# Layer 1's up projection as seven block products instead of eight, from its third pair of column blocks on

## The chip, the cores and the metric

The kernel runs on one core of a Trainium2 chip. The metric is the device time of one execution in microseconds (us). The engines are TensorE (PE, with its weight loads PEld), VectorE (DVE), ScalarE (ACT), GpSimd (POOL) and SyncE (SP), which issues the DMAs. Each has a queue of its own and takes its instructions in the order in which they were written.

## The reference

One step of a network of two layers on 640 tokens (128 context tokens and 512 latent ones), 1024 wide. Each layer is a mixer and then a feed-forward part, which is all that the change touches:

```python
h = rmsnorm(x, p["norm_ffn"]) * (1.0 + sc_f) + sh_f
gate, up = jnp.split(h @ p["w_up"], 2, axis=-1)
x = x + g_f * ((jax.nn.silu(gate) * up) @ p["w_down"])
```

`w_up` is 1024 x 5632 (2816 gate columns, 2816 up columns), `w_down` 2816 x 1024. `sh_f`, `sc_f` and the gate `g_f` come from a small product of a conditioning vector with `ada_w`, one set for the context tokens and one for the latent ones. After layer 1 comes a last rmsnorm, whose result is the output. All is float32.

## The kernel before

**Arithmetic.** A float32 operand is cut into a high part (a rounding copy on ACT) and a low part (a subtraction on DVE). Each product is three matmuls into one accumulator: high by high, high by low, low by high. The normed input of the FFN, transposed, lies in `hT` (high and low, 8 blocks of 128 along k, 640 tokens).

**Weights.** `Stream` brings in one slot of weights after another: `load` is a DMA of up to 512 KB into one of 3 `raw` tiles (L76), `cut` the ACT copy (L86) and the DVE subtraction (L87) into one of 4 pairs `wh`, `wl`. `done` gives a slot back and starts the next cuts and loads.

**Up projection.** `ffn` goes over 22 pairs of column blocks (a gate block and an up block, 128 columns each), in two chunks of 11 pairs in each layer. One block is one slot and 48 matmuls (`ws`, L616): 8 blocks of k, two halves of 320 tokens, 3 matmuls of 128x320. The first three blocks of a layer (L605 to L607) run first over the tokens whose norm is done, then over the rest. A pair ends with ACT's silu (L1080), DVE's product (L1086) and the cut of the result into high and low (L1088, L1089), which makes an `act` tile.

**Down projection.** After each chunk its `act` tiles are multiplied with `w_down`: `cols_512` in matmuls 512 wide (L1035 to L1037), and the last chunk's second half in `as_`, 256 wide (L660 to L662). `x_add` multiplies each result with the gate and adds it to x (L978, L980); the last chunk goes on to the norm and the output (L543 to L556, L1138).

**The gate g_f.** It is computed beside the first chunk by a lane, `ada_gate`, a generator stepped once per 4.0 units of the cost that the main program yields. Per half of the columns it takes 8 tiles of `ada_w` (`adw`, 256 KB, two buffers), each with two DVE instructions of 512 columns, one per conditioning vector (L475 for the first tile, L477 after); then for each vector the cut (ACT L531, DVE L532), two matmuls into `pg` (L535, L536) and the addition to `gate` (L538). `finish("ada", (l, "gf"))` stands before the first down projection of a layer and writes out all that is left of the lane.

**Order.** Each engine runs its instructions in the order in which they were written: `run` draws steps from the main program, the lanes and the pending norms by that cost. Accumulators in PSUM are four tiles of 1024 columns, and a wait stands between whole tiles.

## Time and profile before

| | |
|---|---|
| median of 3 runs | 1823.03 us (1822.45 to 1823.71) |
| the profiled execution, its own time | 1822.63 us |
| its span, first to last instruction | 1820.9 us |
| mean granted TensorE clock | 0.998 |
| busy PE, DVE, ACT | 98%, 57%, 39% |
| layer 1: second part of the first blocks starts | 1358.04 us |
| first chunk's down projection | from 1506.14 us |
| second chunk, up projection | 1582.2 to 1736.4 us |
| last matmul | 1813.28 us |

The profiled execution took 1.7 us more than its span. A row of the timeline gives an instruction's start and its own duration; instructions overlap at their ends, so what one costs in a queue is read from the start of one to the start of the next. "x2" counts instructions put in one row. What stands in brackets is idle time before the row, with what ended it.

### The profile page before, as it was taken

Reading aid. Unit: us, or ns where it says so; the run is one execution under the profiler, and the core shown is the slowest. Engines: PE = TensorE matmul, PEld = TensorE weight load, DVE = VectorE, ACT = ScalarE, POOL = GpSimd, SP = SyncE. Lnnn points to the kernel's source line nnn. Section 1 sums busy time; section 2 is a strip of 40 time slices with the busy share of each in tenths; the row PEclk is TensorE's granted clock in tenths of the full one; section 3 lists DMA queues with packets and bytes.
Section 4 is the critical chain, followed back from the end, with each engine's and each line's share of the span. In section 5 each row is a group of like instructions: output and inputs, shape, how many; then the busy total and the mean of one; then the engine's idle time right before and its main releaser. Section 6 shows DMA issues by size and latency. Waiting matters only on the chain.

```text
span 1820.9 us, 29285 instructions
## 1 busy us (share of the span) xinstructions
PE 1784.9 (98%) x12301; PEld 1714.2 (94%) x12301; DVE 1040.5 (57%) x1613; ACT 715.1 (39%) x1211; POOL 50.7 (3%) x59
## 2 busy tenths in 40 slices
PE   7999999999999999999999999999999999999998
PEld 5999899999999989999899999999899998899988
DVE  6787958855754565555366655687475523323234
ACT  7685445543422212222256455464342221122221
POOL 1100000000000000000000000000000000000000
PEclk9999999999999999999999999999999999999999
DMA  9424233221533444443132111412234422322221
GB/s 343 136 65 148 84 94 110 85 79 47 174 105 100 133 146 132 137 135 116 53 93 74 53 56 53 139 61 91 74 101 122 122 65 75 91 72 74 71 76 59
DMA packets 204612, 184.06 MB, mean 101 GB/s; under 512 B 6736, under 2 KB 172336, under 8 KB 204480
## 3 DMA queue, kind: packets, MB, share of 16 engines
q1 hardware_dynamic: 199584, 179.67, 31.8%
q10 hardware_dynamic: 4640, 2.43, 0.4%
q8 instruction: 96, 1.57, 0.4%
q0 software_dynamic: 256, 0.09, 0.1%
q14 instruction: 36, 0.29, 0.0%
HBM read 177.44 MB, written 4.72 MB: 100 GB/s over the span
## 4 chain that ended last, share of the span: by engine, by line
PE 83%; DVE 8%; ACT 4%; issue 2%; DMA 2%; POOL 1%; SPq 0%; POOLq 0%; DVEq 0%; ACTq 0%
PE gw L616 39%; PE ga L1035 5%; PE ga L1037 5%; PE ga L1036 5%; PE ga L662 5%; PE ga L661 5%; PE ga L660 5%; PE pl L753 3%; DMA adw<-in_ada_w 2%; DVE wl L87 1%; PE gw L606 1%; PE gw L607 1%; PE gw L605 1%; PE ga L1014 1%; PE ga L1013 1%
## 5 line engine op out<-in xcount | busy, mean ns | idle before, releaser
L616 PE MATMUL gw<-hT,wh 128*128 128x320 f32 x3712 | 701.6, 310 | 0.0
L616 PEld LDWEIGHTS gw<-hT,wh 128*128 128x128 f32 x3712 | 581.5, 188 | 1.1
L86 ACT CAST wh<-raw 128x1024 fp32r<-128x1024 f32 (+2 forms) x224 | 231.7, 1035 | 706.7 <-PE gw L616 271.5
L87 DVE TENSOR_TENSOR wl<-raw,wh 128x1024 fp32r<-128x1024 f32 (+2 forms) x224 | 269.4, 1204 | 365.7 <-ACT wh L86 365.5
L616 PE MATMUL gw<-hT,wl 128*128 128x320 f32 x1856 | 423.2, 309 | 0.0
L616 PEld LDWEIGHTS gw<-hT,wl 128*128 128x128 f32 x1856 | 310.4, 188 | 0.1
L660 PE MATMUL ga<-wh,hT 128*128 128x256 f32 x640 | 185.2, 289 | 0.0
L662 PE MATMUL ga<-wh,hT 128*128 128x256 f32 x640 | 181.4, 283 | 0.0
L661 PE MATMUL ga<-wl,hT 128*128 128x256 f32 x640 | 181.2, 283 | 0.0
L1035 PE MATMUL ga<-wh,act 128*128 128x512 f32 x330 | 129.3, 392 | 0.0
L1036 PE MATMUL ga<-wl,act 128*128 128x512 f32 x330 | 128.5, 389 | 0.0
L1037 PE MATMUL ga<-wh,act 128*128 128x512 f32 x330 | 127.8, 389 | 0.0
L1086 DVE TENSOR_TENSOR sgf<-sgf,gw 128x640 f32<-128x640 f32 x44 | 36.1, 821 | 160.5 <-PE gw L616 160.5
L660 PEld LDWEIGHTS ga<-wh,hT 128*128 128x128 f32 x640 | 122.5, 191 | 0.3
L661 PEld LDWEIGHTS ga<-wl,hT 128*128 128x128 f32 x640 | 122.5, 191 | 0.3
L662 PEld LDWEIGHTS ga<-wh,hT 128*128 128x128 f32 x640 | 122.3, 191 | 0.0
L510 DVE CUSTOM_DVE_ANT_0 junk<-adt,srow 128x1024 f32<-128x1024 f32 x96 | 117.2, 1221 | 2.3 <-ACT srow L495 1.1
L477 DVE SCALAR_TENSOR_TENSOR acc<-adw,sTt,acc 128x512 f32<-128x512 f32 x112 | 79.8, 747 | 25.6 <-DMA adw<-in_ada_w 25.5
L753 PE MATMUL pl<-X 128*128 128x128 f32 x560 | 72.9, 277 | 5.1 <-ACT X L740 5.1
L1035 PEld LDWEIGHTS ga<-wh,act 128*128 128x128 f32 x330 | 61.9, 188 | 14.3 <-DVE xa L978 1.9
L753 PEld LDWEIGHTS pl<-X 128*128 128x128 f32 x560 | 67.8, 191 | 7.7 <-ACT X L740 7.1
L1037 PEld LDWEIGHTS ga<-wh,act 128*128 128x128 f32 x330 | 62.0, 188 | 12.9
(227 smaller groups left out, 2623.8 us busy)
## 6 DMA issues: line engine op xcount, KB each, us to landing
raw<-in_w_up SPq DMA_DIRECT2D x88, 512.0 KB, 3.8
raw<-in_w_in SPq DMA_DIRECT2D x72, 512.0 KB, 3.8
adt<-in_ada_t SPq DMA_DIRECT2D x48, 512.0 KB, 3.8
raw<-in_w_down SPq DMA_DIRECT2D x38, 512.0 KB, 3.6
adw<-in_ada_w SPq DMA_DIRECT2D x64, 256.0 KB, 3.2
adw<-in_ada_w SPq DMA_DIRECT2D x16, 512.0 KB, 10.5
raw<-in_w_out SPq DMA_DIRECT2D x16, 512.0 KB, 3.6
gate<-in_ada_b SPq DMA_DIRECT2D x8, 512.0 KB, 5.2
```

Source lines behind the costliest of these rows:

```text
L86: nc.scalar.copy(hi[:, :n], raw[:, :n])
L87: nc.vector.tensor_tensor(lo[:, :n], raw[:, :n], hi[:, :n].bitcast(F32), op=ALU.subtract)
L477: nc.vector.scalar_tensor_tensor(d, w, s, d, op0=ALU.mult, op1=ALU.add)
L510: r = V.tensor_tensor_reduce(out=self.junk, in0=w[:, :DM], in1=self.srow[:, c], scale=1.0, scalar=0.0, op0=ALU.mult, op1=ALU.add, accum_ou ...
L616: mm(o, w[:, k], self.hT[:, d, k, sl], start=k == 0 and i == 0, stop=k == KT - 1 and i == 2)
L660: mm(o, a_hi, hi[:, j], start=i == 0, stop=False)
L661: mm(o, a_hi, lo[:, j], start=False, stop=False)
L662: mm(o, a_lo, hi[:, j], start=False, stop=i == nk - 1)
L753: nc.tensor.matmul(pl[:, i * P:(i + 1) * P], X[:, TOK + i * P:TOK + (i + 1) * P], X[:, i * P:(i + 1) * P], start=True, stop=True)
L1035: mm(o, a_hi, hi[:, j], start=i == 0, stop=False)
L1036: mm(o, a_hi, lo[:, j], start=False, stop=False)
L1037: mm(o, a_lo, hi[:, j], start=False, stop=i == nk - 1)
```

## The change

Layer 0 keeps its two chunks. Layer 1 has five, of 5, 5, 4, 4 and 4 pairs; its first two pairs are as before, the other 20 go through `seven`. There the product of the tokens (two halves of 320), k (two halves of 512) and the two column blocks (gate, up) is put together from seven block products instead of eight: each is 12 matmuls of 128x320, so that a pair has 84 instead of 96.

- **Inputs.** `norm_f` takes the place of `norm_c`: it keeps the float32 input in four tiles `hf`, and takes the third token block, which lies across the halves, in two pieces. `combos` makes four combinations of them on DVE (1280 columns each, L654 to L657) and cuts three (`eh`, ACT L665, DVE L666); `combo_last` cuts the fourth into one quarter of `hT` after the plain pairs.
- **Weights.** A pair is four slots, three of 1024 columns and one of 512. Four DMAs of 256 KB and four DVE sums of 512 columns (`sums`, L112) fill them; the cuts are L103 (ACT) and L104 (DVE), where they were L86 and L87.
- **Results.** Two tiles, `sx` and `sy`, take the products; v2, v3, c22, s2 and c12 (L694 to L709) are DVE instructions of 320 columns, with ACT's copy of the first product (L692), two silus (L702, L705), and the product and cut as before (L712 to L714). Later products of a pair go into the same two tiles.
- **Buffers.** `raw` has 6 tiles; in layer 1 the stream loads up to 6 ahead, in layer 0 three of them hold `srow` and `junk`.

```diff
-CH = (11, 11)
+CH = ((11, 11), (5, 5, 4, 4, 4))
+PLAIN = (NF, 2)
+HK = KT // 2
...
     def load(self):
         src, kk, nn = self.slots[self.loaded]
         raw = self.net.rawp.tile([P, 1024], F32, tag="raw", name="raw")
+        if nn == 0:
+            for c, w in src:
+                self.last = self.net.nc.sync.dma_start(
+                    out=raw[:, c:c + 512].rearrange("p (k n) -> p k n", k=HK), in_=w)
+            self.raw[self.loaded] = (raw, kk, nn)
+            self.loaded += 1
+            return
...
     def cut(self):
         net, nc = self.net, self.net.nc
-        raw, kk, nn = self.raw.pop(self.split)
+        raw, kk, nn = self.raw[self.split]
         n = kk * nn
+        if nn == 0:
+            n = 512 if kk == 3 else 1024
+            self.sums(kk)
+        if nn or kk:
+            self.raw.pop(self.split)
+        if nn == 0 and kk == 1:
+            self.raw.pop(self.split - 1)
...
+    def sums(self, part):
+        add = lambda o, x, y: self.net.nc.vector.tensor_tensor(o, x, y, op=ALU.add)
+        u, v = slice(0, 512), slice(512, 1024)
+        r = lambda i: self.raw[self.split - part + i][0]
+        if part == 0:
+            add(r(1)[:, v], r(0)[:, u], r(3)[:, v])
+            add(r(0)[:, v], r(1)[:, v], r(3)[:, u])
+        elif part == 1:
+            add(r(1)[:, u], r(3)[:, u], r(3)[:, v])
+            add(r(2)[:, v], r(0)[:, v], r(2)[:, u])
...
+            if self.split < self.loaded and self.split < self.used + W_BUFS and self.can_cut():
                 self.cut()
-            elif self.loaded < len(self.slots) and self.loaded < self.split + RAW_BUFS:
+            elif self.loaded < len(self.slots) and self.loaded < self.split + self.depth:
...
-        self.rawp = pool("rawp", RAW_BUFS)
+        self.rawp = pool("rawp", RAW_BUFS + 3)
...
+    def norm_f(self, t, src, l, m):
+        nc = self.nc
+        c = 0 if t == 0 else 1
+        sv = src[:, :DM].rearrange("p (k n) -> p k n", k=KT)
+        G, S = self.modc[:, l, m, 0, c], self.modc[:, l, m, 1, c]
+        a = 0
+        while a < P:
+            h = (t * P + a) // HALF
+            b = min(P, (h + 1) * HALF - t * P)
+            n, o = b - a, t * P + a - h * HALF
+            for kh in range(2):
+                if (h, kh) not in self.F:
+                    self.F[h, kh] = self.B("hf")
+                fv = self.F[h, kh].rearrange("p (k n) -> p k n", k=HK)[:, :, o:o + n]
+                ks = slice(HK * kh, HK * kh + HK)
+                if kh == 0:
+                    for k in range(HK):
+                        nc.scalar.activation(fv[:, k], sv[:, k, a:b], AF.Identity, bias=S[:, k:k + 1],
+                                             scale=G[:, k:k + 1])
+                else:
+                    bc = lambda v: v[:, ks].unsqueeze(2).to_broadcast([P, HK, n])
+                    nc.vector.tensor_tensor(fv, sv[:, ks, a:b], bc(G), op=ALU.mult)
+                    nc.vector.tensor_tensor(fv, fv, bc(S), op=ALU.add)
+                hi, lo = (self.hT[:, d, ks, t * P + a:t * P + b] for d in range(2))
+                nc.scalar.copy(hi, fv)
+                nc.vector.tensor_tensor(lo, fv, hi.bitcast(F32), op=ALU.subtract)
+            a = b
...
+    def combos(self):
+        V, F = self.nc.vector, self.F
+        V.tensor_tensor(F[1, 0], F[1, 1], F[1, 0], op=ALU.subtract)
+        V.tensor_tensor(F[0, 0], F[0, 0], F[1, 0], op=ALU.add)
+        V.tensor_tensor(F[1, 1], F[0, 0], F[1, 1], op=ALU.subtract)
+        V.tensor_tensor(F[0, 1], F[0, 0], F[0, 1], op=ALU.subtract)
+        self.E = {}
+        for n, q in ((2, (0, 0)), (1, (1, 0)), (4, (0, 1))):
+            self.E[n] = [self.B("eh", F32R).rearrange("p (k t) -> p k t", k=HK) for _ in range(2)]
+            self.combo(q, *self.E[n])
+
+    def combo(self, q, hi, lo):
+        f = self.F.pop(q).rearrange("p (k t) -> p k t", k=HK)
+        self.nc.scalar.copy(hi, f)
+        self.nc.vector.tensor_tensor(lo, f, hi.bitcast(F32), op=ALU.subtract)
+
+    def combo_last(self):
+        self.E[3] = self.quarter(1, 0)
+        self.combo((1, 1), *self.E[3])
+
+    def seven(self, act):
+        nc, W, E = self.nc, self.W, self.E
+        mm, V = nc.tensor.matmul, nc.vector
+        X, Y, T = self.ps("sx"), self.ps("sy"), self.ON("sv")
+        x0, x1, y0, y1 = X[:, :HALF], X[:, 512:512 + HALF], Y[:, :HALF], Y[:, 512:512 + HALF]
+        v2, v3, c12, c22 = (T[:, i * HALF:(i + 1) * HALF] for i in range(4))
+        sg = self.B("sgf")
+        s1, s2 = sg[:, :HALF], sg[:, HALF:TOK]
+
+        def prod(o, w, j, h, first=True):
+            hi, lo = (x[:, HK * j:HK * j + HK] for x in w)
+            for k in range(HK):
+                mm(o, hi[:, k], h[0][:, k], start=first and k == 0, stop=False, skip_group_check=True)
+                mm(o, hi[:, k], h[1][:, k], start=False, stop=False, skip_group_check=True)
+                mm(o, lo[:, k], h[0][:, k], start=False, stop=k == HK - 1, skip_group_check=True)
+            if j:
+                W.done()
+            return 5.1e-3 * HALF
+        a = W.get(W.used)
+        yield prod(x0, a, 0, self.quarter(0, 0))
+        nc.scalar.copy(v2, x0)
+        yield prod(x1, a, 1, E[2])
+        V.tensor_tensor(v2, x1, v2, op=ALU.subtract)
+        b = W.get(W.used)
+        yield prod(y0, b, 0, E[3])
+        V.tensor_tensor(v3, v2, y0, op=ALU.subtract)
+        yield prod(y1, b, 1, E[1])
+        V.tensor_tensor(c22, v3, y1, op=ALU.subtract)
+        c = W.get(W.used)
+        yield prod(x0, c, 0, self.quarter(0, 1), False)
+        nc.scalar.activation(s1, x0, AF.Silu)
+        yield prod(x1, c, 1, self.quarter(1, 1))
+        V.tensor_tensor(s2, x1, v3, op=ALU.subtract)
+        nc.scalar.activation(s2, s2, AF.Silu)
+        d = W.get(W.used)
+        cost = prod(y1, d, 0, E[4], False)
+        W.done()
+        V.tensor_tensor(c12, v2, y1, op=ALU.subtract)
+        at = self.B("act", F32R).rearrange("p (d t) -> p d t", d=2)
+        fv = sg[:, TOK:]
+        V.tensor_tensor(fv, sg[:, :TOK], T[:, TOK:], op=ALU.mult)
+        nc.scalar.copy(at[:, 0], fv)
+        V.tensor_tensor(at[:, 1], fv, at[:, 0].bitcast(F32), op=ALU.subtract)
+        act.append(at)
+        yield cost
...
-        for ci, nch in enumerate(CH):
-            last = ci == len(CH) - 1
+        f0 = 0
+        for ci, nch in enumerate(CH[l]):
+            last = ci == len(CH[l]) - 1
             act = []
+            plain = min(nch, max(0, PLAIN[l] - f0))
+            f0 += nch
...
-            evs = [e for f in range(nch) for e in pair()]
+            evs = [e for f in range(plain) for e in pair()]
             if ci == 0:
                 yield from self.ws(*evs[:3], mid=mid)
                 evs = evs[3:]
+                if PLAIN[l] < NF:
+                    self.combos()
             for e in evs:
                 yield from self.ws(e)
+            if ci == 0 and PLAIN[l] < NF:
+                self.combo_last()
+            for _ in range(plain, nch):
+                yield from self.seven(act)
...
+                    self.W.depth = RAW_BUFS + 3
```

On DVE, at the turn from the plain pairs to the first of seven, before the change (L87 weight cuts, L477 gate lane, L1086 and L1089 the end of a pair):

```order
L1086 TENSOR_TENSOR sgf_12944<-sgf_12944,gw_12831 128x640
L87 TENSOR_TENSOR wl_12975<-raw_12827,wh_12974 128x1024
L1089 TENSOR_TENSOR act_12980<-sgf_12944,act_12980 128x640
L477 SCALAR_TENSOR_TENSOR acc_12868<-adw_13020,sTt_126,acc_12868 128x512
L477 SCALAR_TENSOR_TENSOR acc_12868<-adw_13061,sTt_126,acc_12868 128x512 x2
L87 TENSOR_TENSOR wl_13013<-raw_12829,wh_13012 128x1024
L477 SCALAR_TENSOR_TENSOR acc_12868<-adw_13100,sTt_126,acc_12868 128x512 x2
L477 SCALAR_TENSOR_TENSOR acc_12868<-adw_13128,sTt_126,acc_12868 128x512 x2
```

And after it (L666 is the low part of a combination, L512 the lane's L477, L104 the weight cut, L1224 and L1227 the end of the plain pair, L112 a weight sum, L694 the first result of the first pair of seven):

```order
L666 TENSOR_TENSOR eh_13058<-hf_12503,eh_13057 128x1280
L512 SCALAR_TENSOR_TENSOR acc_12884<-adw_13098,sTt_126,acc_12884 128x512
L104 TENSOR_TENSOR wl_13115<-raw_12644,wh_13114 128x512
L1224 TENSOR_TENSOR sgf_13039<-sgf_13039,gw_13061 128x640
L666 TENSOR_TENSOR hT_12378<-hf_12764,hT_12378 128x4x320
L1227 TENSOR_TENSOR act_13119<-sgf_13039,act_13119 128x640
L512 SCALAR_TENSOR_TENSOR acc_12884<-adw_13141,sTt_126,acc_12884 128x512 x2
L112 TENSOR_TENSOR raw_12847<-raw_12845,raw_12998 128x512
L694 TENSOR_TENSOR sv_13127<-sx_13125,sv_13127 128x320
```

The last two of eight instructions of 1280 columns are seen here. The one that writes `hT` (the low part of E3, 4 blocks of 320) stands behind the lane, a weight cut and the second plain pair's product, and ahead of it on DVE stand the other seven.

On DVE, the end of the gate lane, before: in the middle of the first chunk's eleven pairs.

```order
L477 SCALAR_TENSOR_TENSOR acc_13341<-adw_13535,sTt_126,acc_13341 128x512
L477 SCALAR_TENSOR_TENSOR acc_13341<-adw_13564,sTt_126,acc_13341 128x512 x2
L477 SCALAR_TENSOR_TENSOR acc_13341<-adw_13615,sTt_126,acc_13341 128x512 x2
L87 TENSOR_TENSOR wl_13528<-raw_13335,wh_13527 128x1024
L532 TENSOR_TENSOR hl_13643<-acc_13341,hl_13643 128x512
L1086 TENSOR_TENSOR sgf_13533<-sgf_13533,gw_13539 128x640
L87 TENSOR_TENSOR wl_13593<-raw_13403,wh_13592 128x1024
L1089 TENSOR_TENSOR act_13598<-sgf_13533,act_13598 128x640
L87 TENSOR_TENSOR wl_13659<-raw_13468,wh_13658 128x1024
L538 TENSOR_TENSOR gate_12864<-gate_12864,pg_13691 128x512
```

And after: at the end of the chunk of five (L512 is the lane's accumulation, L568 its low part and L574 the addition, as L477, L532 and L538 were; L714 ends the last pair, L104 is the next weight cut).

```order
L714 TENSOR_TENSOR act_13533<-sgf_13407,act_13533 128x640
L512 SCALAR_TENSOR_TENSOR acc_13439<-adw_13549,sTt_126,acc_13439 128x512
L512 SCALAR_TENSOR_TENSOR acc_13439<-adw_13553,sTt_126,acc_13439 128x512 x2
L512 SCALAR_TENSOR_TENSOR acc_13439<-adw_13557,sTt_126,acc_13439 128x512 x2
L568 TENSOR_TENSOR hl_13561<-acc_13439,hl_13561 128x512
L574 TENSOR_TENSOR gate_12880<-gate_12880,pg_13564 128x512
L568 TENSOR_TENSOR hl_13568<-acc_13439,hl_13568 128x512
L574 TENSOR_TENSOR gate_12882<-gate_12882,pg_13571 128x512
L104 TENSOR_TENSOR wl_13594<-raw_13373,wh_13593 128x1024
```

Five of the lane's accumulations and both of its cuts now follow the last pair of the chunk.

On PE, the entry to the first down projection, before:

```order
L616 MATMUL gw_14141<-hT_12371,wh_13958 128x320 x4
L616 MATMUL gw_14141<-hT_12371,wl_13959 128x320 x2
L1035 MATMUL ga_14200<-wh_14017,act_12980 128x512
L1036 MATMUL ga_14200<-wl_14018,act_12980 128x512
L1037 MATMUL ga_14200<-wh_14017,act_12980 128x512
```

And after (L571 and L572 are the lane's two matmuls, L1170 to L1172 the down projection):

```order
L685 MATMUL sy_13405<-eh_13058,wh_13393 128x320
L686 MATMUL sy_13405<-eh_13057,wl_13394 128x320
L571 MATMUL pg_13564<-hl_13561,onesr_89 128x512
L572 MATMUL pg_13564<-hl_13561,onesr_89 128x512
L571 MATMUL pg_13571<-hl_13568,onesr_89 128x512
L1170 MATMUL ga_13575<-wh_13433,act_13001 128x512
L572 MATMUL pg_13571<-hl_13568,onesr_89 128x512
L1171 MATMUL ga_13575<-wl_13434,act_13001 128x512
L1172 MATMUL ga_13575<-wh_13433,act_13001 128x512
```

Both pairs of the lane's matmuls now stand at the head of the down projection; the first down-projection matmul lies between them.

## Rows read from the trace of the kernel before

**Rows 1.** Windows: stretch; busy us of PE, PEld, DVE, ACT, POOL; PEclk; DMA.

```profile
1582.00:1736.00 154.00, 154.00 (x1051) 153.96 (x1051) 43.82 (x46) 36.66 (x43) 0.00 (x0) 1.00 0.25 74
...
1814.00:1821.00 7.00, 0.00 (x0) 0.00 (x0) 2.17 (x6) 0.51 (x2) 0.55 (x1) 0.69 0.39 151
```

**Rows 2.** Chain of waits, layer 1's up projection: start, us, what.

```profile
1358.20 0.52 PE gw L605 x3
...
1371.15 20.68 PE gw L616 x141
...
1582.22 154.14 PE gw L616 x1051
```

**Rows 3.** Waits of PE, 1305 to 1821 us: total, times, longest.

```profile
PE pt L562 <- DVE xn L1057: 0.8, 2, 0.6
```

**Rows 4.** Timeline of DVE, layer 1's up projection: start, us, instruction, idle before.

```profile
1360.28 1.41 DVE L477 SCALAR_TENSOR_TENSOR acc<-adw,sTt,acc 128x512 f32<-128x512 f32 x2
1363.21 1.42 DVE L477 SCALAR_TENSOR_TENSOR acc<-adw,sTt,acc 128x512 f32<-128x512 f32 x2 [1.52 <-DMA adw<-in_ada_w]
1364.54 1.22 DVE L87 TENSOR_TENSOR wl<-raw,wh 128x1024 fp32r<-128x1024 f32 x1
1365.68 1.41 DVE L477 SCALAR_TENSOR_TENSOR acc<-adw,sTt,acc 128x512 f32<-128x512 f32 x2
...
1378.63 0.69 DVE L532 TENSOR_TENSOR hl<-acc,hl 128x512 fp32r<-128x512 f32 x1
1379.23 0.81 DVE L1086 TENSOR_TENSOR sgf<-sgf,gw 128x640 f32<-128x640 f32 x1
```

**Rows 5.** Groups by shape, DVE and ACT: busy us, mean ns, idle before.

```profile
L728 DVE TENSOR_TENSOR QQ<-F,QS 128x1280 f32<-128x1280 f32 x8 | 11.9, 1488 | 0.1
...
L86 ACT CAST wh<-raw 128x1024 fp32r<-128x1024 f32 x214 | 224.6, 1050 | 662.4 <-PE gw L616 251.0 <-issue 185.9 <-PE ga L1037 181.3
```

**Rows 6.** DMA issues: count, KB each, median us to landing.

```profile
adw<-in_ada_w SPq DMA_DIRECT2D x64, 256.0 KB, 3.2
```

**Rows 7.** Timeline: two hand-overs between PE and DVE.

```profile
1391.66 0.39 PE L535 MATMUL pg<-hl,onesr 128*128 128x512 f32 x1
...
1391.93 0.82 DVE L1086 TENSOR_TENSOR sgf<-sgf,gw 128x640 f32<-128x640 f32 x1 [5.05 <-PE gw L616]
...
1576.80 0.68 DVE L978 TENSOR_TENSOR xa<-ga,gate 128x512 f32<-128x512 f32 x1
...
1577.54 0.19 PEld L1035 LDWEIGHTS ga<-wh,act 128*128 128x128 f32 x1 [0.25 <-DVE xa L978]
```

**Rows 8.** Timeline of PE, first down projection.

```profile
1506.61 0.39 PE L1037 MATMUL ga<-wh,act 128*128 128x512 f32 x1
1506.84 0.40 PE L1035 MATMUL ga<-wh,act 128*128 128x512 f32 x1
```

**Rows 9.** Windows and timeline of PE, where the clock is low.

```profile
42.00:44.00 2.00, 2.00 (x8) 2.00 (x8) 1.84 (x5) 2.00 (x5) 0.00 (x0) 0.50 1.07 378
...
41.07 0.33 PE L605 MATMUL gw<-hT,wh 128*128 128x384 f32 x1
...
42.38 0.52 PE L605 MATMUL gw<-hT,wh 128*128 128x384 f32 x1
```

**Rows 10.** Timeline of the end: DVE and PE's last.

```profile
1809.64 0.43 DVE L978 TENSOR_TENSOR xa<-ga,gate 128x256 f32<-128x256 f32 x1
...
1812.23 1.29 DVE L1138 SCALAR_TENSOR_TENSOR y<-x,rs,nf 128x1024 f32<-128x1024 f32 x1 [0.73 <-POOL rs L556]
...
1813.28 0.28 PE L662 MATMUL ga<-wh,act 128*128 128x256 f32 x1
...
1813.60 0.42 DVE L978 TENSOR_TENSOR xa<-ga,gate 128x256 f32<-128x256 f32 x1
...
1815.12 0.16 DVE L551 TENSOR_REDUCE tot<-ssq 128x1 f32<-128x3 f32 x1 [0.63 <-ACT xa L543]
...
1816.19 1.41 DVE L1138 SCALAR_TENSOR_TENSOR y<-x,rs,nf 128x512 f32<-128x512 f32 x2 [0.73 <-POOL rs L556]
```

More of the change, by code (lines that the diff above doesn't have):

```diff
@@ L71, in __init__ @@
         self.raw, self.ready = {}, {}
+        self.depth = RAW_BUFS
     def load(self):
@@ L87, in cut @@
         nc.vector.tensor_tensor(lo[:, :n], raw[:, :n], hi[:, :n].bitcast(F32), op=ALU.subtract)
+        if nn == 0:
+            kk = n // P
         self.ready[self.split] = (hi[:, :n].rearrange("p (k n) -> p k n", k=kk),
@@ L90, in cut, with can_cut @@
         self.split += 1
+    def sums(self, part):
[8 more added lines that the diff above has]
+            add(r(2)[:, v], r(0)[:, v], r(2)[:, u])
+    def can_cut(self):
+        src, kk, nn = self.slots[self.split]
+        return self.loaded >= self.split + 4 or nn != 0 or kk != 0
     def pump(self):
         while True:
-            if self.split < self.loaded and self.split < self.used + W_BUFS:
+            if self.split < self.loaded and self.split < self.used + W_BUFS and self.can_cut():
                 self.cut()
-            elif self.loaded < len(self.slots) and self.loaded < self.split + RAW_BUFS:
+            elif self.loaded < len(self.slots) and self.loaded < self.split + self.depth:
                 self.load()
@@ L134, in __init__ @@
         self.srow = None
+        self.F = {}
         self.pendT = []
@@ L482, in ada_rows @@
         a = self.a
-        self.srow = self.const.tile([P, 2, DM], F32, name="srow")
-        self.junk = self.const.tile([P, DM], F32, name="junk")
+        self.srow = [self.rawp.tile([P, 1024], F32, tag="raw", name="srow") for _ in range(2)]
+        self.junk = self.rawp.tile([P, 1024], F32, tag="raw", name="junk")
         for c, src in enumerate((a["c_ctx"], a["c"])):
             with self.tc.issue_after(self.W.last.ins):
-                self.nc.sync.dma_start(out=self.srow[:, c], in_=bass.AP(src.tensor, src.offset, [[0, P], [1, DM]]))
+                self.nc.sync.dma_start(out=self.srow[c], in_=bass.AP(src.tensor, src.offset, [[0, P], [1, DM]]))
     def ada_cols(self, l, m, alloc):
@@ L494, in ada_cols @@
                 yield
-            self.pin(self.nc.scalar.activation(self.srow, self.srow, AF.Silu))
+            for c in range(2):
+                self.pin(self.nc.scalar.activation(self.srow[c], self.srow[c], AF.Silu))
         tiles = [(which, j) for which in (1, 0) for j in range(KT)]
@@ L509, in ada_cols @@
             for c in range(2):
-                r = V.tensor_tensor_reduce(out=self.junk, in0=w[:, :DM], in1=self.srow[:, c], scale=1.0, scalar=0.0,
+                r = V.tensor_tensor_reduce(out=self.junk, in0=w[:, :DM], in1=self.srow[c], scale=1.0, scalar=0.0,
                                            op0=ALU.mult, op1=ALU.add,
@@ L566, in norm_c @@
         nc = self.nc
+        if m == 1 and PLAIN[l] < NF:
+            return self.norm_f(t, src, l, m)
         km = KT // 2
@@ new lines, in quarter @@
+    def quarter(self, h, kh):
+        return [self.hT[:, d, HK * kh:HK * kh + HK, h * HALF:(h + 1) * HALF] for d in range(2)]
+    def combos(self):
[8 more added lines that the diff above has]
+            self.combo(q, *self.E[n])
@@ L1157, in as_, with seven @@
                 out.append((w[r:r + kk * P, c:c + 256].rearrange("(k p) n -> p k n", p=P), kk, 256))
+        def seven(w, cg, cu):
+            q = lambda kh, c: w[kh * 512:kh * 512 + 512, c:c + P].rearrange("(k p) n -> p k n", p=P)
+            for part, src in enumerate(([(0, q(0, cg))], [], [(0, q(1, cg))], [(0, q(1, cu)), (512, q(0, cu))])):
+                out.append((src, part, 0))
         def c512(w, r0, nk, c):
@@ L1178, in slots @@
             f0 = 0
-            for nch in CH:
+            for nch in CH[l]:
                 for f in range(f0, f0 + nch):
-                    ws(wu, f * P)
-                    ws(wu, DFF + f * P)
+                    if f < PLAIN[l]:
+                        ws(wu, f * P)
+                        ws(wu, DFF + f * P)
+                    else:
+                        seven(wu, f * P, DFF + f * P)
                 c512(wd, f0 * P, nch, 0)
```

## The prediction

> **What bounds the kernel now.** I read first the windows over layer 1, then the chain of waits, PE's waits, and only then DVE's timeline. The windows show PE busy without a gap in the second chunk's up projection and DVE in 43.82 of 154 us [rows 1]. The chain lies on PE there: 1051 matmuls of 128x320 in 154.14 us, 146.7 ns each [rows 2]. From the FFN of layer 1 to the end PE waits for other engines practically nowhere; its longest wait is 0.6 us, in the norm ahead of it [rows 3]. So each matmul taken out is worth its 146.7 ns, as long as the other engines keep the next one fed. The reader should keep DVE in view: the change takes work from PE and gives a good deal to DVE, and does so in the one chunk where DVE already serves the lane for g_f.
>
> **What is removed.** 20 pairs with 12 matmuls less each: 240 x 146.7 ns = 35.2 us. The last chunk is 4 pairs instead of 11, so 7 blocks go from the 256-wide form to the 512-wide one: 7 x 5 tiles x 3 = 105 matmuls of 0.23 us [rows 8] for 210 of 0.12 us (33 of them lie between two results at the end, 1813.60 - 1809.64 = 3.96 us [rows 10]): 24.2 for 25.2, 1.0 us gained. Together 36.2 us.
>
> **DVE's prices.** From start to start: 1024 columns 1.14 us (1364.54 to 1365.68), 512 columns 0.60 (1378.63 to 1379.23), a lane accumulation 1.33 / 2 = 0.67 (1363.21 to 1364.54) [rows 4]. The straight line through the first two gives estimates of 0.40 for 320, 0.74 for 640 and 1.41 for 1280 columns; the nearest row for 1280 has 1.49 us of own duration [rows 5] where 1024 has 1.22 [rows 4], so it bears the estimate out. The 1280 and 320 forms could lie 10% to either side.
>
> **The first chunk, as work.** From the start of the second part of the first blocks (1358.20; call it 0) PE has 13 us (to 1371.15 [rows 2]), one block of 48 (7.0) and three pairs of seven (36.9): 57 us. In the order of DVE there stand, up to the lane's last low part but one: 8 of 1280 columns (11.3), 32 of the lane (21.4), 11 cuts of 1024 and 5 of 512 (15.5), 8 weight sums (4.8), 15 results of 320 (6.0), 10 of 640 (7.4), and 6 of 512 from norm, low parts and gate (3.6): 70 us. DVE is the bound of this chunk by 13 us even if it never waits. The lower end of the loss is therefore 13 us.
>
> **The first chunk, as waits.** A walk through the order with these prices, a product's end to DVE 0.27 us (1391.66 to 1391.93), DVE's end to PE about 0.1 (1576.80 + 0.68 to 1577.54) [rows 7], and a copy of 1024 on ACT 1.05 [rows 5]:
> - The first pair of seven starts at 20.2 on PE; its second product ends at 23.8. The next, from the quarter of `hT` that is written over, needs E3's low part. Its DVE instruction stands behind the other combinations, the lane and three weight cuts, and ends at 26.7: PE waits 3.0. v2 then comes at 29.8 behind two lane accumulations and a sum: 1.5 more.
> - The lane's first matmuls stand in PE's order amid the next pair at 38.8; their low part comes after four weight cuts, four sums and the first pair's product, at 43.0: 4.4. In the second pair 0.7 for v2, and 3.1 for the lane's second pair of matmuls (55.0 against 58.1). In the third 0.8.
> - At the end PE is through with the third pair at 71.8. The down projection's first matmuls stand behind the lane's last ones. On DVE the lane's second half begins only at 64. Its 8 tiles go through two buffers: a tile given back at 1360.28 is replaced and used at 1363.21, after 1.52 us of waiting [rows 4]; the DMA itself takes 3.2 us [rows 6]. I take 3.3 from release to use, as the tiles also stand in SP's queue behind weight loads that wait for DVE's own cuts. Two tiles are there at first; six more come in three turns of 3.3 + 1.35, the later ones held up by the pair's own results: the last accumulation ends at 83.7. Cut on ACT, low part, matmuls, gate and the second low part follow: 87.1. PE waits 14.6 us.
>
> The sum is 28.1 us. Ahead of it, `norm_f` (two pieces of the third token block), two weight sums and the first combination stand before the last low part of `hT`, three of 0.6 and 1.41 less what was idle: 2 us (0.5 to 4). So 30.1 us, between 13 (only DVE's work counts) and 38 (each reload 1 us longer, which makes 3 us in the three turns, and 5 us more in the waits between, by the 10% on DVE's estimated forms and the lane's tiles there). I stay with the walk, since the lane waited for its tiles already before.
>
> **The clock.** Where PE had little to do, around 42 us, the granted clock is 0.50 for two us, and matmuls of 384 columns take 0.52 instead of 0.33 [rows 9]; behind the last matmul, with PE idle, its mean is 0.69 [rows 1]. That is 1.2 of 2.4 GHz. After the wait of 14.6 us I take one such stretch. The two rows put it between 2 us at half speed, which costs 1.0, and the loss of 0.31 over 7 us, 2.2: I take 1.7 us. Bounds: 0, and 5 with two more such stretches. The Trainium skill ("TensorE: Matmul & The Clock Gate", Part 1) says that an idle array falls to 1.2 GHz and that only sustained work lifts it again. By that rule the shorter waits could cost the same; it is a rival below.
>
> **The steady pairs.** The other 17 pairs have 9.9 us of DVE work (cuts 4.0, sums 2.4, results 2.0, product and low part 1.5) beside 12.3 of PE, so DVE stays ahead, and loads have the spare time before the cuts. But a product may enter `sx` or `sy` only when the whole tile was read. Between first and second product stand 4 matmuls, 0.59 us, against 0.27 + an ACT copy of 320 columns (0.33 in proportion to 1.05 us, more with a fixed part) + the return: 0.8. So 0.2 to 0.3 there; the other results have 8 to 12 matmuls (1.2 to 1.8 us) of cover against 0.8, and up to 1.1 more where a cut of 1024 stands ahead. I take 0.3 per pair, 5.1 us; bounds 0 (hidden) and 10.
>
> **More ends of chunks.** Three more passages from a down projection to the next pairs, each with a wait like the 0.25 for xa [rows 7] and a result behind the last additions: 0.5 each, 1.5 us (0 to 4).
>
> **The end.** In the last chunk a result comes each 12 x 0.12 = 1.44 us instead of 3.96. DVE needs per token block two of about 0.45, two short ones (0.16) and y, 1.29 [rows 10]: 2.7 us. Five blocks are 13.3 us from 1.44 x 4 = 5.8 us before PE's end: 7.6 behind it, where y now ends at 1816.19 + 1.41, 4.0 behind (1813.28 + 0.28). The last two blocks' chains over ACT and POOL add some 2.5 as y of the block before stands between them. 6 us (3 to 7.5).
>
> **Sum.** -36.2 + 30.1 + 1.7 + 5.1 + 1.5 + 6.0 = +8.2. On the profiled execution's own 1822.63 us (span 1820.9 and 1.7 around it; 0.4 below the median shown) that is 1830.8; I say 1831. Layer 0 keeps its order but for a few neighbours, for which I take 0 (1 us either way).
>
> **Rivals.**
> - *DVE's work hides.* The lane's tiles come in time and only the excess of 13 us remains, the clock stays at 2.4 GHz, the pairs lose 0.1 each: -36.2 + 13 + 2 + 2 + 1 + 4 = -14.2, about 1808. For it: DVE has gaps while it waits for products, where the lane fits, and three of my waits rest on estimated forms. Against it: both low parts stand behind the last pair in the order, and two buffers leave the lane no way to start early.
> - *The clock falls at every wait above 3 us,* three more times: 3 x 1.7 = 5.1, 1836. For it the clock in rows 9; against it, these waits are a fifth to a third as long as the one at the end, with matmuls before and after. The page's rule, carried to this chunk, would give this time.
> - *The pairs themselves wait.* If in each steady pair one result stands behind a cut of 1024 columns that waits itself, 1.14 us x 17 = 19 more: 1850. It decides where the cover falls under 0.8 + 1.1 us. Against it: DVE has 2.4 us to spare in each pair.
> - *The sums meet near nothing:* the lane loses 8 instead of 14.6 us, all else as forecast: 1824.
>
> **Chances.** Forecast 0.44 (with its own range 1826 to 1839), hidden 0.27, clock 0.08, pairs 0.10, near nothing 0.11. A measurement of this kernel can tell about 0.2%, 3.6 us, from no change. Faster 0.27, same 0.11, slower 0.44 + 0.08 + 0.10 = 0.62. The range runs from just below the hidden case, 1806, to between forecast and waiting pairs, 1846.
>
> **What would show it.** PE waits on `pg` L571 ahead of the first L1170 for 10 us or more, with DVE's L512 waiting for `adw` beside it; a wait of L685 on `sy` for L666 of some 3 us; PEclk at 0.5 behind the long wait; steady pairs of 12.5 to 12.8 us; y ending 9 to 11 us after the last matmul. I am wrong if the entry to the first down projection has no wait above 5 us, or if a steady pair takes over 13.5 us.

## The result

| | before | changed |
|---|---|---|
| median of 4 runs | 1823.06 us (1822.45 to 1823.71) | 1840.44 us (1836.80 to 1842.85) |
| profiled execution, own time | 1822.63 us | 1836.80 us |
| its span | 1820.9 us | 1835.0 us |
| last matmul begins | 1813.28 us | 1822.35 us |

The ratio of the times is 1.0094, with a 95% interval of 1.0076 to 1.0111: slower by 17.4 us, where 8.2 were forecast. The profiled execution is the fastest of the four; its own difference is 14.2 us, and the rest is looked for below among the executions.

The windows of the changed kernel follow the columns of [rows 1]: stretch, busy us of PE, PEld, DVE, ACT and POOL, then PEclk and DMA. They are the first chunk's three pairs of seven, its down projection, the second chunk's five pairs, and the stretch behind the last matmul.

```profile
1378.00:1447.00 69.00, 45.98 (x262) 41.31 (x261) 53.06 (x77) 21.32 (x32) 0.00 (x0) 0.89 0.33 103
1447.00:1485.00 38.00, 38.00 (x158) 30.76 (x158) 21.14 (x30) 5.27 (x5) 0.00 (x0) 0.93 0.10 28
1485.00:1549.00 64.00, 63.57 (x417) 60.89 (x416) 46.61 (x70) 26.88 (x39) 0.00 (x0) 1.00 0.31 95
1823.00:1835.00 12.00, 0.00 (x0) 0.00 (x0) 6.73 (x15) 0.91 (x4) 1.65 (x3) 0.70 0.47 186
```

PE was never short of work in these places before. Now it works 46 of 69 us in the first stretch, at a mean clock of 0.89, and DVE is the busiest engine there. In the third, PE is busy again almost without a gap, so what is lost in the steady pairs isn't visible in a busy share. The last stretch has DVE at work for 6.7 of 12 us with nothing on PE; from the last matmul's start to the end it is 12.7 us, and it was 7.6 before.

PE's four largest waits from 1305 us on, in us in total, times and longest (before, the longest was 0.7):

```profile
PE pg L571 <- ACT hl L567: 17.6, 4, 10.7
PE pt L598 <- DVE xn L1192: 3.4, 3, 2.5
PE sx L684 <- DVE sv L694: 3.0, 6, 1.2
PE sy L685 <- DVE hT L666: 2.7, 1, 2.7
```

The four waits on `pg` are the lane for g_f; the row of `sx` is v2, the one of `sy` is E3's low part, written into `hT`. The largest, 10.7 us, stands ahead of the first down projection. In the timelines of DVE and of PE there (start, us, instruction, idle before):

```profile
1438.85 0.81 DVE L714 TENSOR_TENSOR act<-sgf,act 128x640 fp32r<-128x640 f32 x1
1439.59 0.74 DVE L512 SCALAR_TENSOR_TENSOR acc<-adw,sTt,acc 128x512 f32<-128x512 f32 x1
1441.16 1.42 DVE L512 SCALAR_TENSOR_TENSOR acc<-adw,sTt,acc 128x512 f32<-128x512 f32 x2 [0.83 <-DMA adw<-in_ada_w]
1443.03 1.41 DVE L512 SCALAR_TENSOR_TENSOR acc<-adw,sTt,acc 128x512 f32<-128x512 f32 x2 [0.45 <-DMA adw<-in_ada_w]
1444.46 0.69 DVE L568 TENSOR_TENSOR hl<-acc,hl 128x512 fp32r<-128x512 f32 x1
```

```profile
1433.44 0.31 PE L686 MATMUL sy<-eh,wl 128*128 128x320 f32 x1
1444.48 0.79 PE L571 MATMUL pg<-hl,onesr 128*128 128x512 f32 x1 [10.73 <-ACT hl L567]
1445.21 0.79 PE L572 MATMUL pg<-hl,onesr 128*128 128x512 f32 x1
1446.71 0.80 PE L571 MATMUL pg<-hl,onesr 128*128 128x512 f32 x1 [0.71 <-ACT hl L567]
1447.30 0.63 PE L1170 MATMUL ga<-wh,act 128*128 128x512 f32 x1
1447.73 0.63 PE L572 MATMUL pg<-hl,onesr 128*128 128x512 f32 x1
1448.15 0.63 PE L1171 MATMUL ga<-wl,act 128*128 128x512 f32 x1
```

PE begins the last matmul of its products at 1433.44. DVE is still at the lane's tiles, of which it has to wait 0.45 and 0.83 us for a DMA, and ends the accumulation at 1444.4. The matmuls behind it then run at half the rate: from 1447.30 to 1447.73 and on to 1448.15 it is 0.43 us for 512 columns where 0.23 is the rate of [rows 8].

### The profile page after: what moved, and what is told of

The parts are those of the page before. It is cut to its first block, busy times and chain, and to the rows that moved or that the text cites. A ratio compares the mean times of both kernels' runs of the same rounds, so it can differ in the third digit from the quotient of the medians.

```text
span 1835.0 us, 29181 instructions
## 1 busy us (share of the span) xinstructions
PE 1767.5 (96%) x11956; PEld 1676.0 (91%) x11956; DVE 1215.7 (66%) x1905; ACT 764.0 (42%) x1302; POOL 50.6 (3%) x59
## 4 chain that ended last, share of the span: by engine, by line
PE 78%; DVE 12%; ACT 5%; issue 3%; DMA 1%; POOL 1%; SPq 0%; DVEq 0%; POOLq 0%; ACTq 0%
PE gw L751 24%; PE ga L1170 6%; PE ga L1172 6%; PE ga L1171 6%; PE ga L797 4%; PE ga L796 4%; PE ga L795 4%; PE pl L888 3%; PE sx L684 2%; PE sx L685 2%; PE sx L686 2%; DVE wl L104 2%; PE sy L684 2%; PE sy L685 2%; PE sy L686 1%
## 5 line engine op out<-in xcount | busy, mean ns | idle before, releaser
L103 ACT CAST wh<-raw 128x1024 fp32r<-128x1024 f32 (+1 forms) x264 | 264.9, 1004 | 630.6 <-PE ga L1172 212.1
L104 DVE TENSOR_TENSOR wl<-raw,wh 128x1024 fp32r<-128x1024 f32 (+1 forms) x264 | 306.4, 1166 | 258.0 <-ACT wh L103 256.2
L751 PE MATMUL gw<-hT,wh 128*128 128x320 f32 x2432 | 461.9, 311 | 0.0
L751 PEld LDWEIGHTS gw<-hT,wh 128*128 128x128 f32 x2432 | 380.5, 188 | 0.6
L751 PE MATMUL gw<-hT,wl 128*128 128x320 f32 x1216 | 277.2, 309 | 0.0
L751 PEld LDWEIGHTS gw<-hT,wl 128*128 128x128 f32 x1216 | 203.1, 188 | 0.0
L1170 PE MATMUL ga<-wh,act 128*128 128x512 f32 x365 | 145.2, 398 | 0.1
L1172 PE MATMUL ga<-wh,act 128*128 128x512 f32 x365 | 141.3, 392 | 0.0
L1113 DVE TENSOR_TENSOR xa<-ga,gate 128x512 f32<-128x512 f32 (+1 forms) x110 | 62.8, 589 | 41.6 <-PE ga L1172 17.8
L512 DVE SCALAR_TENSOR_TENSOR acc<-adw,sTt,acc 128x512 f32<-128x512 f32 x112 | 79.6, 746 | 15.2 <-DMA adw<-in_ada_w 15.2
L1170 PEld LDWEIGHTS ga<-wh,act 128*128 128x128 f32 x365 | 69.1, 189 | 18.7 <-DVE xa L1113 4.9
L1172 PEld LDWEIGHTS ga<-wh,act 128*128 128x128 f32 x365 | 69.1, 189 | 14.8
L1171 PEld LDWEIGHTS ga<-wl,act 128*128 128x128 f32 x365 | 69.1, 189 | 13.2
L684 PE MATMUL sx<-hT,wh 128*128 128x320 f32 x240 | 76.5, 322 | 3.3 <-DVE sv L694 3.0
```

Source lines behind the costliest of these rows:

```text
L103: nc.scalar.copy(hi[:, :n], raw[:, :n])
L104: nc.vector.tensor_tensor(lo[:, :n], raw[:, :n], hi[:, :n].bitcast(F32), op=ALU.subtract)
L512: nc.vector.scalar_tensor_tensor(d, w, s, d, op0=ALU.mult, op1=ALU.add)
L684: mm(o, hi[:, k], h[0][:, k], start=first and k == 0, stop=False, skip_group_check=True)
L751: mm(o, w[:, k], self.hT[:, d, k, sl], start=k == 0 and i == 0, stop=k == KT - 1 and i == 2)
L1170: mm(o, a_hi, hi[:, j], start=i == 0, stop=False)
```

## Where the 14.2 us come from

Each stretch of the profiled execution is set against that of before, by the times at which the kinds of matmuls change on PE:

| stretch | forecast | measured |
|---|---|---|
| matmuls left out and wider form | -36.2 | -36.5 |
| up to the first pair of seven | +2.0 | +0.6 |
| waits in the first chunk's three pairs | +28.1 | +23.0 |
| low clock and hand-overs there, and in the down projection behind | +1.7 | +10.1 |
| 17 steady pairs | +5.1 | +9.8 |
| later down projections and passages | +1.5 | +2.1 |
| behind the last matmul | +6.0 | +5.1 |
| sum | +8.2 | +14.2 |

The three pairs take from 1378.18 to 1447.30, 69.1 us, where 252 matmuls and seven of the lane's eight would take 38.6; 23.0 of the 30.5 are waits, 7.5 are not. The down projection takes 37.0 instead of 34.4 (with the lane's eighth), nearly all of it in its beginning at half clock. A steady pair takes 12.9 us (chunks 2 to 5: 64.7 us for five pairs, 51.5 for four) instead of 12.32.

The 0.6 us up to the first pair of seven are two things. From the first matmul of layer 1's up projection to the first of seven it takes 33.3 us, where the same 192 matmuls and what lies between took 31.3: 2.0 us, as forecast. But that first matmul comes 1.45 us earlier than before (1344.87 instead of 1346.32), chiefly because of layer 0's first matmuls, which the change leaves alone. Their window before and in the changed kernel:

```profile
40.00:64.00 24.00, 24.00 (x156) 23.98 (x156) 15.75 (x43) 17.22 (x30) 3.29 (x1) 0.93 0.59 197
40.00:64.00 24.00, 24.00 (x169) 23.98 (x169) 16.03 (x44) 18.79 (x33) 3.29 (x1) 1.00 0.83 265
```

In this execution the clock there was at 1.00, before at 0.93, and in the second trace of the changed kernel, below, it is at 0.93 again.

## Experiments

All times are medians of runs beside the kernel before on the same chip; before took 1821.4 to 1821.8 us there, the changed kernel 1839.5 to 1840.4.

**The changed kernel again.**

> The changed kernel once more, to see which of its stretches differ between executions. Theory (the clock falls after the waits of the first chunk, and how often differs from one execution to the next): the span moves with the time at 1.2 GHz while PE works, 1836 to 1843 us, and the waits of the first chunk stay within 1 us of those seen. Rival (the waits themselves differ, as the gate lane's tiles land sooner or later): the same times, but the wait ahead of the first down projection moves by 3 us or more at the same share of low clock.

Measured: 1839.46 us (ratio 1.0096, 1.0081 to 1.0111). The waits are the same to 0.2 us, but for v2 (1.9 instead of 3.0 in total), and the one ahead of the down projection is 10.8 again. The clock isn't the same. Windows of this run, and then of the first profile (columns as above):

```profile
1386.00:1400.00 14.00, 13.53 (x71) 12.97 (x71) 11.32 (x18) 4.47 (x6) 0.00 (x0) 0.78 0.31 92
1420.00:1430.00 10.00, 9.82 (x46) 9.29 (x47) 4.15 (x8) 1.80 (x4) 0.00 (x0) 0.69 0.22 81
```

```profile
1386.00:1400.00 14.00, 10.68 (x69) 9.79 (x67) 12.60 (x21) 4.49 (x6) 0.00 (x0) 1.00 0.37 108
1420.00:1430.00 10.00, 9.71 (x60) 9.15 (x59) 4.66 (x10) 1.79 (x3) 0.00 (x0) 0.92 0.22 65
```

From 1386 to 1400 us the second execution ran at 0.78 of the clock, the first at 1.00; the three pairs took 71.6 us instead of 69.1, and the down projection behind them 36.2 instead of 37.0. So the theory holds for these two traces: they differ in how much of the first chunk runs at 1.2 GHz. The Trainium skill ("TensorE: Matmul & The Clock Gate", Part 1) says of the start of a kernel that the number of slow matmuls differs from run to run; these two traces show the same of a stretch in its middle (0.78 against 1.00).

**Five chunks, all pairs plain.**

```diff
-PLAIN = (NF, 2)
+PLAIN = (NF, NF)
```

> Layer 1 in five chunks, but all 22 pairs plain, so with the work of before on PE but for the form of 7 blocks. Theory (the chunks cost their ends, about 1.5 us, the output behind the last matmul about 5, and the lane squeezed into five pairs some 2; the form gives 1 back): 1830 us. Rival (the pairs of seven carry all of the loss): 1823 to 1825 us.

Measured: 1841.29 us (1.0107, 1.0092 to 1.0122), against both. Five chunks alone cost as much as the whole change. PE waits 8.9 and 0.7 us on `pg` ahead of the down projection, and 13.3 us lie behind the last matmul's start, where it was 7.6. I had put the lane at 2 us here, because DVE has room in a plain chunk; but the lane's end doesn't come from DVE's load: around the long wait DVE itself stands still, 2.6 and 2.0 us, for the lane's tiles.

**The first chunk plain, 17 pairs as seven.**

> The first chunk of layer 1 all plain (5 pairs), the other 17 pairs as seven products. Theory (the first chunk is where the gain is lost, because DVE has 70 us of work beside 57 us of PE there; with plain pairs PE has 71 us): 204 matmuls less are 29.9 us, 1 from the form, against 17 x 0.57 for the steady pairs, 5 at the end, 1.5 at chunk ends and some 2 to 4 for the lane: 1808 to 1813 us, faster than before. Rival (the seven-product pairs and the chunks lose it wherever they stand, the first chunk's waits only move on): 1825 us or more.

The edit is `PLAIN = (NF, 5)`. Measured: 1820.09 us (0.9987, 0.9978 to 0.9997), 20 us below the changed kernel though three pairs fewer have seven products, so the first chunk is where most was lost. It isn't 1810, since the lane's wait stays (7.9 and 0.7 us), as in the run before.

**A short lane.** The kernel leaves out 7 of the 8 tiles of each half of layer 1's g_f.

```diff
-        for k in range(KT):
+        for k in range(1 if l == 1 and col >= 5120 else KT):
```

> The changed kernel with layer 1's gate lane cut to the first of its 8 tiles per half (the gate is left incomplete; 14 DMAs and 28 DVE accumulations are not done). Theory (DVE's work decides the first chunk, and the lane is what stands behind the last pair): DVE has 51 us beside 57 of PE, the waits on the lane's matmuls (17.6 us in the profile) and most low-clock stretches go: 1815 to 1820 us. Rival (the combinations and results of the seven-product pairs hold PE up on their own): the waits on v2 and E3 stay and grow, 1830 us or more.

Measured: 1814.44 us (0.9954, 0.9937 to 0.9971), 25 us below the changed kernel; E3's wait is gone, and of the waits on `pg` 3.4 us are left of 17.6. With 28 x 0.67 = 19 us less on DVE its work fits. But 14 DMAs of the lane are gone as well, so this run doesn't tell DVE's load from the lane's tiles.

**The lane earlier.**

```diff
-            self.run(self.ffn(l, True), {"ada": Q_ADA[2]})
+            self.run(self.ffn(l, True), {"ada": Q_ADA[2] if l == 0 else 2.0})
```

> The changed kernel with layer 1's gate lane stepped once per 2.0 of cost instead of 4.0 during its FFN: the same lane, spread over the first chunk, so that its last matmuls stand within the third pair of seven. Theory (DVE has 13 us more to do in that chunk than PE, wherever the lane stands): the 10.8 us ahead of the down projection go, but waits on E3, v2 and the lane's matmuls grow by some 3 to 5 in their place, and one stretch of low clock goes: 1828 to 1833 us. Rival (only the late step of the lane costs, DVE has room): all waits on the lane's matmuls go and 4 to 6 us of low clock with them: 1815 to 1820 us.

Measured: 1834.59 us (1.0071, 1.0057 to 1.0084), 5.8 us below the changed kernel. The wait ahead of the down projection is gone, but 3.8 us for v2's copy and 3.8 twice for `pg` stand in its place earlier, and the first pair of seven starts 8.7 us later. Over the chunk PE waits 16.8 us instead of 23.0: of the 11.4 us that go, 5.2 come back. The wait moves, as it does in a chunk in which DVE has more to do than PE.

**The lane earlier, all pairs plain.** The same edit with 2.5, on the five plain chunks.

> All pairs plain in five chunks, with the lane stepped once per 2.5 of cost instead of 4.0 in layer 1's FFN. Theory (the lane has some 25 steps of 4.0 and the first chunk of five pairs ends before them, so the lane's tiles are fetched one after another while PE waits 9.6 us): the wait goes, and 2 to 3 us of low clock with it, leaving the output behind the last matmul (5.7) and the chunk ends: 1828 to 1830 us. Rival (the lane is bound by its tiles through two buffers however it is stepped): the wait shrinks by less than half, 1836 us or more.

Measured: 1827.68 us (1.0035, 1.0022 to 1.0048). No wait on `pg` is left. So in a plain chunk it was the lane's step alone: the chunk of five pairs ends before the lane's steps do, and `finish` puts what is left behind the last pair.

**PE kept busy in the long wait.** The kernel computes 60 matmuls more, which nothing reads.

```diff
+            if ci == 0 and PLAIN[l] < NF:
+                D = self.ps("dm")
+                for i in range(60):
+                    nc.tensor.matmul(D[:, :HALF], self.onesr, self.hT[:, 0, 0, :HALF], start=i == 0, stop=i == 59)
```

> The changed kernel with 60 more matmuls of 128x320 (8.8 us, into a tile that nothing reads) between the last pair of seven of the first chunk and the lane's matmuls. Theory (the long wait costs itself and then a slow stretch: the matmuls behind it run at half speed for some 7 us): the wait shrinks to 1 to 2 us, its end stays where it is, and the slow stretch behind it goes: 3 to 4 us less than the changed kernel, 1836 us. Rival (the clock behind the wait is of no weight): the same time, 1839 to 1841 us, or more where the wait was shorter than 8.8 us.

Measured: 1839.38 us (1.0098, 1.0084 to 1.0112), 1 us below the changed kernel and no different. The waits and the windows in this stretch:

```profile
PE pg L571 <- ACT hl L567: 3.3, 2, 2.6
```

```profile
1436.00:1445.00 9.00, 8.79 (x60) 8.52 (x59) 8.07 (x13) 2.04 (x4) 0.00 (x0) 1.00 0.72 222
1445.00:1450.00 5.00, 1.67 (x3) 0.85 (x4) 3.74 (x6) 1.24 (x2) 0.00 (x0) 0.80 0.04 16
1450.00:1460.00 10.00, 10.00 (x35) 8.00 (x35) 3.64 (x6) 1.05 (x1) 0.00 (x0) 0.76 0.01 2
```

The long wait is down to 2.6 us and the clock stays at 1.00 up to 1445 us; but behind the 2.6 us it is low all the same, 0.80 and then 0.76. So it isn't the length of the long wait that costs the slow stretch behind it; what it costs beside itself was not shown by this run. My theory of the clock falls in this form.

**The products of a pair in the two tiles in turn.** Products 1, 3, 5 and 6 go to `sx`, 2, 4 and 7 to `sy`, and the seventh runs before the sixth.

```diff
-        yield prod(x1, a, 1, E[2])
-        V.tensor_tensor(v2, x1, v2, op=ALU.subtract)
+        yield prod(y0, a, 1, E[2])
+        V.tensor_tensor(v2, y0, v2, op=ALU.subtract)
...
-        yield prod(y0, b, 0, E[3])
-        V.tensor_tensor(v3, v2, y0, op=ALU.subtract)
+        yield prod(x1, b, 0, E[3])
+        V.tensor_tensor(v3, v2, x1, op=ALU.subtract)
```

> The changed kernel with the products of a pair written to the two tiles in turn (1, 3, 5, 6 in one, 2, 4, 7 in the other, the seventh ahead of the sixth), so that every product has 12 matmuls between it and the reading of its tile. Theory (the 0.57 us that a steady pair takes over its 84 matmuls are waits on whole tiles): a pair takes 12.4 to 12.5 us instead of 12.9, 6 to 8 us in all: 1833 us. Rival (each product that follows a hand-over from another engine loses about 0.1 us even when nothing is late): pairs of 12.8 us or more, 1838 to 1841 us.

Measured: 1828.49 us (1.0037, 1.0024 to 1.0049), 12 us below the changed kernel, where 6 to 8 were expected. The second chunk's up projection, from its first matmul to the first of the down projection behind it, before the change of tiles and after it (0.9 us of the same work stand ahead of each):

```profile
1485.16 0.30 PE L684 MATMUL sx<-hT,wh 128*128 128x320 f32 x1
...
1548.94 0.39 PE L1170 MATMUL ga<-wh,act 128*128 128x512 f32 x1
```

```profile
1483.55 0.30 PE L684 MATMUL sx<-hT,wh 128*128 128x320 f32 x1
...
1545.15 0.39 PE L1169 MATMUL ga<-wh,act 128*128 128x512 f32 x1
```

64.7 us against 62.5 for five pairs: 12.9 against 12.5 us for each. Of the 8.8 us between the two profiled executions, 17 x 0.43 = 7.3 are that; where the medians' further 3 us come from isn't shown. In the changed kernel a product whose tile comes free too late loses 0.1 to 0.2 us even where no wait is listed. Here is the second product of the second pair, on ACT and on PE:

```profile
1499.04 0.43 ACT L692 COPY sv<-sx 128x320 f32<-128x320 f32 x1 [0.22 <-PE sx L686]
1499.28 0.31 PE L684 MATMUL sy<-hT,wh 128*128 128x320 f32 x1
1499.52 0.41 PE L684 MATMUL sx<-eh,wh 128*128 128x320 f32 x1
1499.77 0.31 PE L685 MATMUL sx<-eh,wh 128*128 128x320 f32 x1
1499.92 0.30 PE L686 MATMUL sx<-eh,wl 128*128 128x320 f32 x1
```

ACT has read the tile at 1499.47. The product was due at 1499.43 and starts at 1499.52, and its second matmul follows 0.25 us after the first, where 0.147 is the rate: 0.19 us lost, the same in all five pairs. With 12 matmuls between, it is gone from most of these places. The rival, that each hand-over costs 0.1 whatever stands between, is refuted.

**The three edits together, and the size of the last chunk.** The first chunk plain, the lane stepped at 2.5, the tiles in turn; then the same with other chunks.

```diff
-CH = ((11, 11), (5, 5, 4, 4, 4))
+CH = ((11, 11), (5, 3, 4, 4, 6))
```

> Three edits together: the first chunk of layer 1 plain (17 pairs as seven), the lane stepped once per 2.5 of cost in layer 1's FFN, and the products of a pair in the two tiles in turn. Theory (the loss is made of the first chunk, the lane's late end, the whole-tile waits, and the output): from the five plain chunks with the early lane, 1827.7, 17 pairs of 12.5 instead of 14.08 us take 26.9: 1801 us, 1.1% faster than before. Rival (with the gains of a pair back, DVE's work for combinations and sums shows in the first chunk or at its end): 1808 us or more.

Measured: 1802.71 us (0.9896, 0.9882 to 0.9909), as the theory has it. Its first chunk and its second chunk's pairs:

```profile
1354.00:1422.00 68.00, 67.73 (x444) 66.19 (x443) 56.60 (x72) 25.31 (x33) 0.00 (x0) 1.00 0.40 125
1458.00:1519.00 61.00, 61.00 (x412) 60.13 (x411) 45.75 (x69) 26.41 (x38) 0.00 (x0) 1.00 0.32 100
```

DVE has 57 of 68 us in the first chunk, and PE no gap that matters, though all the combinations are made there.

> The three edits with chunks of 5, 3, 4, 4 and 6 pairs. Theory (the output lags because a result comes each 12 x 0.12 = 1.44 us and DVE needs about 2.7 for each of the five token blocks): with 6 pairs a result comes each 2.16 us, the lag behind the last matmul shrinks by 4 x 0.72 = 2.9 us: 1798 us. Rival (the lag is the chain over ACT and POOL, the same for any chunk): as e8, 1801 us.

Measured: 1799.64 us (0.9883, 0.9868 to 0.9898), 3.1 below; 10.2 us lie behind the last matmul's start where e8 has 12.5. Between the profiles the lag shrinks by 2.3 us, where the theory had 2.9. It is the fastest kernel of this study, faster than both that were given.

> The three edits with chunks of 5, 5, 5, 5 and 2 pairs. Theory of the output's lag: a result comes each 0.72 us, so the lag grows by up to 4 x 0.72 = 2.9 us, while the form of two more blocks gives 0.3 back: 1803 to 1804 us. Rival: as e8, 1801 us.

Measured: 1808.49 us (0.9927, 0.9915 to 0.9940), 5.8 above e8 where 2 to 3 more were expected. 15.9 us lie behind the last matmul's start, 3.5 more, and PE itself is held up:

```profile
PE ga L794 <- DVE xa L1112: 2.1, 3, 0.9
```

The lag grows about as the theory has it (by up to 2.9); that the next results wait for DVE's `xa` to read the tile `ga` is a second price that I had not seen.

> The changed kernel (20 pairs as seven) with the lane stepped once per 2.0 and the products in the two tiles in turn. Theory (both losses are apart): 1840 - 5.5 - 11.5 = 1823 us, about as before, 20 us or more above e8, all in the first chunk, where DVE has more to do than PE. Rival (with the tiles' waits gone DVE catches up in the first chunk): 1812 us or less.

Measured: 1822.46 us (1.0007, 0.9998 to 1.0016), as the theory has it and as long as before; 20 us above e8, with 36 matmuls less. Its waits in the first chunk:

```profile
PE pg L571 <- ACT hl L567: 7.7, 3, 4.0
PE sx L684 <- ACT sv L692: 4.1, 2, 3.1
PE sy L684 <- DVE sv L694: 2.3, 2, 2.0
```

Nothing is left of the wait at the end of the chunk, and yet 14 us of waits stand in it, on the lane, v2 and its copy.

## Why the prediction came out as it did

**Right:** the side, and where the loss lies. With the first chunk plain (e2, e8) the gain comes back, with the lane earlier (e4, e11) the waits in good part only move. The places of the walk were right one by one: 2.7 us for E3 (3.0 forecast), 1.2 for v2 (1.5), 2.6 and 3.6 for the lane's matmuls (4.4 and 3.1), and the long one ahead of the down projection. That one is 11.4 with its second part instead of 14.6, chiefly because PE came to it 3.6 us later than in the walk (1433.6 - 1358.2 = 75.4 instead of 71.8), while the lane's second half, once begun, took 18.4 us instead of 19.7.

**How far DVE's load goes.** Windows from the walk's start to the lane's last tile in the changed kernel, and of the three pairs of seven in e4:

```profile
1358.20:1444.50 86.30, 63.98 (x381) 60.06 (x379) 70.88 (x97) 29.80 (x40) 0.00 (x0) 0.93 0.34 107
1386.90:1446.30 59.40, 46.40 (x258) 43.19 (x257) 42.52 (x63) 17.15 (x26) 0.00 (x0) 0.89 0.30 93
```

DVE works 70.9 us in the first, as forecast (70), beside the 57 that PE's matmuls need: its load is the floor of 13 to 14 us that the prediction gave. The rest isn't load: in the changed kernel's three pairs DVE itself stands still for 16 of 69 us, in e4's for 17 of 59, and in e8 it works 57 of 68 us without holding PE up. That the rest comes from the order of DVE's queue, where one instruction that waits holds up those behind it, is how the walk got its waits, and it fits all runs; but no run changes that order alone, so it is argued and not shown.

**Wrong: two terms were too small.** "I take 0.3 per pair, 5.1 us" was 0.57 and 9.8 us, and a pair took 12.9 us where 12.5 to 12.8 was the sign. The second product, which is the one that I had priced, loses 0.19. The other 0.38 is lost at products whose 8 to 12 matmuls of cover I had taken to be enough: the instruction that they need, most often a reading of the tile, ends only about 0.05 us ahead of them, in one place 0.5 us after they were due, and their second matmul comes 0.1 late. e7 takes 0.43 per pair away by tiles and order alone.

The other is "After the wait of 14.6 us I take one such stretch", 1.7 us with bounds 0 and 5. Matmuls ran at half the rate behind three of the waits, and not in the same places in each execution:

```profile
1401.20:1404.30 3.10, 3.10 (x13) 3.00 (x12) 2.01 (x4) 0.57 (x2) 0.00 (x0) 0.50 0.02 8
1418.20:1421.40 3.20, 3.20 (x10) 2.67 (x11) 2.09 (x3) 0.55 (x1) 0.00 (x0) 0.50 0.60 230
1444.50:1452.00 7.50, 6.79 (x15) 4.69 (x16) 2.69 (x4) 0.62 (x1) 0.00 (x0) 0.50 0.00 0
```

PE works 13.1 us at 0.50 there, so of the 10.1 us for low clock and hand-overs in and behind the first chunk an estimate of 6.5 is the clock. That was in the main the rival on the clock, which I had given 0.08 and 5.1 us; waits of 2.6 and 3.6 us were enough, as e6 shows too. The term isn't independent of the waits: what makes PE later in the pairs makes the long wait shorter, since the lane ends it. Waits, clock and hand-overs of that chunk together are 33.1 us, where 28.1 + 1.7 were forecast.

**Luck.** The profiled execution won 1.45 us in layer 0, at a clock that was low there in the profile of before; without that its difference would have been 15.6 instead of 14.2. The walk's waits were 5.1 us too long and the end 0.9, which hid part of the two terms. Of the 3.2 us between the profiled execution and the median, 2.1 show in the second trace, chiefly in a layer 1 that starts 0.6 later and a first chunk that takes 1.7 more with its down projection.

**A step that was right for half of its reasons.** I put the wait ahead of the down projection down to DVE's load and to the lane's two buffers. In the changed kernel that load is there, but e1 has the wait (8.9 us) without it, and e5 takes it away by the step of the lane: drawn at a fixed step, the lane isn't done when a chunk of five pairs ends, and its last tiles then come one after another through the two buffers. Both causes are in the changed kernel: e4 removes the step's, and 5.2 us of the 11.4 come back as waits elsewhere.

**One thing told ahead of the prediction is inexact:** PE's order in the changed program isn't that of the source throughout. Four matmuls of the third product stand ahead of the second, which is why the cover there was 0.59 us and not less.

**Left open:** how the 3.6 us that are left of the 10.1 divide among the hand-overs; what order of DVE's queue would bring the first chunk down to DVE's load; and what the long wait does to the clock by itself, which e6 didn't settle.

## What to carry to other kernels

When work is taken from the engine that sets the time, add up what the change gives to the others stretch by stretch, and above all in the stretch where something else already runs beside; an average share (57% DVE) says nothing of it. A lane that is drawn at a fixed step must be drawn faster when the stretch beside it gets shorter, or its rest falls in front of whoever waits for it. And where results of a chain go into few accumulators, alternate them, so that a whole product lies between a result and the next write to its tile.
